# TensorE's order fixed to the program's in the two differential-attention layers of a five-stage fp32 block

## The chip, the cores and the metric

One core of a Trainium2 chip runs the whole program. The metric is the device time of one execution in microseconds (us); lower is better. Batch is 1, the sequence 512 tokens, the model width 1024, all fp32.

## What is computed

Six stages in a row, each adding to the stream `x` (512 x 1024): differential attention, a Conformer convolution, latent attention, differential attention again (with its own weights), a mix of three branches, and a gated feed-forward. The change touches the first and the fourth, which run the same code:

```python
def _diff_attention(h, w_in, q_g, k_g, lq1, lk1, lq2, lk2, sub_g, w_out, lambda_init):
    q, k, v, gate = split(h @ w_in)              # h = rms_norm(x, g)
    q = _apply_rope(_rms_norm(q, q_g), cos, sin) # 8 heads, 2 maps of 64 each
    k = _apply_rope(_rms_norm(k, k_g), cos, sin)
    for s0 in range(0, seq, QBLOCK):             # 4 query blocks of 128
        s = einsum('bhmqd,bhmkd->bhmqk', q[s0:e], k[:e]) * scale
        p = _chunk_causal_softmax(s, s0)
        wts = p[:, :, 0] - lam * p[:, :, 1]
        outs.append(einsum('bhqk,bhkd->bhqd', wts, v[:e]))
    o = _rms_norm(concat(outs), sub_g) * (1.0 - lambda_init)
    return (o * silu(gate)) @ w_out
```

## The kernel before

**Products.** Every large product is made of three fp32r matmuls (`mm3`, L356: high by high, high by low, low by high), each with a moving side of 512 columns. Text below calls one `mm3` a product. A weight unit (512 KB) comes by DMA from the queue of SP (L52), ScalarE rounds it to its high part (L53), and VectorE or GpSimd subtracts to get the low part (L60). Three raw buffers and six pairs of high and low are in turn.

**An attention layer** (`layer_a`, L509) goes through four pairs of heads. For a pair, `project` (L567) first runs the q and k product for four token blocks t = 0 to 3, eight `mm3` each, with the four weight units outside and the token outermost (`tok_outer`), so a token needs all four units. Its result goes through `qk` (L571): a copy and a square on ScalarE (L573, L574), a sum on VectorE (L576), rotary embedding on GpSimd (`rope`, L458 to L461, four instructions), the reciprocal root on GpSimd (L223, L217), and a scaling on VectorE (L580). Only then can `turn` (L582) transpose it on TensorE (four transposes into a PSUM bank `lin`), and ScalarE and VectorE split the result into q and k (L353, L354). A second product gives v and the gate (`vg`, L596). Before its last token, `begin` (L606) asks for all four turns and starts the attention of the pair: for each query block and head the scores (`sc`), the softmax (L637, L638), the transposes of the weights (`weights`, L649), their copy (L652), the values (`values`, L655) and, when both heads are there, `finish` (L668) with two GpSimd instructions (L673, L217) and an output turn (L677). These steps run between the products of the next pair. `out_proj` (L700) multiplies by `w_out`; its last part goes token by token and begins the next layer's norm (`norm`, L325, then `turn`, L341).

**What sets the order.** The program is emitted with the help of `Flow` (L99): a clock that counts matmul columns and a heap of steps with due times. After each `mm3`, `pump` (L115) emits the steps that are due; `need` (L119) emits steps early when something cannot go on without them. Due times are constants: a turn of q and k comes 14 after its token's products in the first pair and 10 + 2t in the others (`A_FIRST`, `A_TURN`), an output turn `A_OUT` = 8.5 after the values, a norm's turn `NORM` = 5 after the norm. A planner that simulates the engines then orders each engine's instructions anew: it takes what it holds to be ready, in order of priority, so that the order emitted is a wish and not a rule. In layer B alone one stretch is kept in the emitted order on TensorE.

PSUM has eight banks: four `lin`, two `tp`, two `sc`. At the start of the kernel seven groups of transposes keep TensorE busy until the first token of `x` has come (`WARM`), and the norms of all four tokens are emitted at once.

Of the kernel before, what the change touches and what calls it, by code (L numbers as in the profile page):

```python
# [13 lines left out]
ALU = mybir.AluOpType  # L14
# [12 lines left out]
NORM = 5.0  # L27
# [3 lines left out]
class WeightStream:  # L31
# [3 lines left out]
    def __init__(self, k, depth, bufs_raw, bufs_hl):  # L35
        self.k, self.depth = k, depth
        self.units, self.made, self.at, self.begun = [], {}, 0, 0
        self.raw = k.ctx.enter_context(k.tc.tile_pool(name="wraw", bufs=bufs_raw))
        self.hl = k.ctx.enter_context(k.tc.tile_pool(name="whl", bufs=bufs_hl))
        self.turn = 0  # L40
# [58 lines left out]
class Flow:  # L99
# [2 lines left out]

    def __init__(self):
        self.clock, self.heap, self.n = 0.0, [], 0

    def later(self, us, fn):
        self.n += 1
        heapq.heappush(self.heap, (self.clock + us, self.n, fn))
# [4 lines left out]
        fn()  # L113

    def pump(self):  # L115
        while self.heap and self.heap[0][0] <= self.clock:
            self._pop()

# [28 lines left out]
class K:  # L147
# [174 lines left out]
            accum_out=self.sums[t][:, b : b + 1],  # L322
        )

    def norm(self, t):  # L325

        nc = self.nc
        x = self.x[:, t]
        s2, ms = self.sums[t], self.stat(1)
        nc.gpsimd.tensor_scalar(out=ms, in0=s2[:, 0:1], scalar1=s2[:, 1:2], scalar2=EPS, op0=ALU.add, op1=ALU.add)  # L330
        r = self.power(ms)
        for b in range(2):
            f = slice(512 * b, 512 * b + 512)
            if b == 1 and t in self.on_pool:
                nc.scalar.activation(out=x[:, f], in_=x[:, f], func=AF.Copy, scale=r)
                nc.gpsimd.tensor_tensor(out=x[:, f], in0=x[:, f], in1=self.gain[:, f], op=ALU.mult)
            else:
                nc.vector.scalar_tensor_tensor(out=x[:, f], in0=x[:, f], scalar=r, in1=self.gain[:, f], op0=ALU.mult, op1=ALU.mult)
        self.flow.later(NORM, lambda: self.turn(t))

    def turn(self, t):  # L341
        if self.newh is None:
# [106 lines left out]
                nc.gpsimd.tensor_tensor(out=cs[:, :, i, a], in0=cos, in1=over(g[:, i, a]), op=ALU.mult)  # L449
                nc.gpsimd.tensor_tensor(out=sn[:, :, i, a], in0=(neg, sin)[half], in1=over(g[:, i, b]), op=ALU.mult)  # L450

    def rope(self, m, raw, tmp, cs, sn, n, groups):

        nc = self.nc
        v = lambda a: a.rearrange("p (i g d) -> p i g d", i=n, g=groups)
        bc = lambda a: a.unsqueeze(2).to_broadcast([P, n, groups, a.shape[-1]])
        rv, mv, tv = v(raw), v(m), v(tmp)
        nc.gpsimd.tensor_tensor(out=tv[..., 0:32], in0=rv[..., 32:64], in1=bc(sn[..., 0:32]), op=ALU.mult)  # L458
        nc.gpsimd.tensor_tensor(out=tv[..., 32:64], in0=rv[..., 0:32], in1=bc(sn[..., 32:64]), op=ALU.mult)
        nc.gpsimd.tensor_tensor(out=mv, in0=rv, in1=bc(cs), op=ALU.mult)  # L460
        nc.gpsimd.tensor_tensor(out=m, in0=m, in1=tmp, op=ALU.add)  # L461

    def add_x(self, n, last=True, scale=1.0, norm=True):
        def consume(t, ps):
# [20 lines left out]
A_SPACE = (1.6, 0.004)  # L485
A_WEIGHTS = (3.5, 0.0065)
A_READY = 1.6
A_OUT = 8.5
A_POOL = 0.3
START_NORM = ()  # L490
WARM = 7
START_LOAD = (2, 5)
A_NORM = (1, 2, 3)


def units_a(ins, j):
    w, wo = ins["a_w_in"][j], ins["a_w_out"][j]
    out = []
    for p in range(4):
        c = 256 * p  # L500
        out += units_tm(w, [(c, 256), (1024 + c, 256)])
        out += units_tm(w, [(2048 + c, 256), (3072 + c, 256)])
    for half in range(2):
        for n in range(2):
            out += units_tm(wo, [(512 * n, 512)], 4 * half, 4)
    return out


def layer_a(k, j, li, gnext, out=None, start=False):  # L509
    nc, tc, ins, flow = k.nc, k.tc, k.ins, k.flow  # L510
    k.share(A_POOL)
    with ExitStack() as ctx:
# [4 lines left out]
        def wt(n, bufs, nmn):  # L517
            return work.tile([P, n], F32, tag=nmn, name=k.nm(nmn), bufs=bufs)

        if start:  # L520

            def between(t):
                if t == 0:
                    k.begin_norm(ins["a_norm_g"][j : j + 1, :], START_NORM)
                    k.share(0.0)
                    k.ws.ahead(START_LOAD[0])
                elif t == 1:
                    k.ws.ahead(START_LOAD[1])
                    k.share(A_POOL)

            k.load_x(between)

            for _ in range(WARM):
                k.transposes([k.ident] * 4)
            for t in range(NT):
                for b in range(2):
                    k.squares(t, b)
                k.norm(t)


        cs = one.tile([P, NT, 2, 64], F32, tag="cs", name=k.nm("cs"))
        sn = one.tile([P, NT, 2, 64], F32, tag="sn", name=k.nm("sn"))
# [24 lines left out]
        def project(p):  # L567

            ks[p] = one.tile([P, 2, 2, S], F32R, tag="ks", name=k.nm("ks"), bufs=2)

            def qk(t, ps):  # L571
                m = wt(512, 4, "m2")
                nc.scalar.activation(out=m, in_=ps, func=AF.Copy)  # L573
                nc.scalar.activation(out=ps, in_=ps, func=AF.Square)  # L574
                ss = k.stat(8)
                nc.vector.tensor_reduce(out=ss, in_=ps.rearrange("p (g d) -> p g d", d=64), axis=AX.X, op=ALU.add)  # L576
                k.rope(m, m, wt(512, 2, "t2"), cs[:, t], sn[:, t], 2, 4)
                r = k.rstd(ss, 64)
                mv = m.rearrange("p (g d) -> p g d", d=64)
                nc.vector.tensor_tensor(out=mv, in0=mv, in1=r.unsqueeze(2).to_broadcast([P, 8, 64]), op=ALU.mult)  # L580

                def turn():  # L582
                    tp = k.transposes([m[:, c * P : (c + 1) * P] for c in range(4)], "lin")
                    s = slice(t * P, (t + 1) * P)
                    q = one.tile([P, 2, 2, 2, P], F32R, tag="qs", name=k.nm("qs"), bufs=4)
                    a, b = slice(0, 64), slice(64, 128)
                    for m_, u, v in ((0, a, b), (1, b, a)):
                        k.split(tp[u, 2:4], ks[p][u, m_, :, s], ks[p][v, m_, :, s])
                        k.split(tp[u, 0:2], q[u, 0, m_], q[u, 1, m_])
                        nc.gpsimd.tensor_copy(out=q[v, :, m_], in_=q[u, :, m_])  # L590
                    qs[p, t] = q
                    turned.add((p, t))

                flow.later(A_FIRST if p == 0 else A_TURN[0] + A_TURN[1] * t, turn)

            def vg(t, ps):  # L596
                vt[p, t] = wt(256, 4, "vt")
                sg[p, t] = wt(256, 4, "sg")
                nc.scalar.activation(out=vt[p, t], in_=ps[:, :256], func=AF.Copy)
                th = wt(256, 2, "th")  # L600
                nc.scalar.activation(out=th, in_=ps[:, 256:], func=AF.Tanh, scale=0.5)
                nc.vector.scalar_tensor_tensor(out=sg[p, t], in0=th, scalar=1.0, in1=ps[:, 256:], op0=ALU.add, op1=ALU.mult)  # L602

            k.lin_tm(k.h_opnd, 8, qk, tok_outer=True, first=p == 0)

            def begin():  # L606
                flow.need(lambda: all((p, t) in turned for t in range(NT)))
                if p % 2 == 0:
                    pair = k.big(F32R, "ot") if p == 0 else one.tile([P, 4096], F32R, tag="ot", name=k.nm("ot"))
                    pair = pair.rearrange("p (i r h t) -> p i r h t", i=2, r=2, h=2)  # L610
                    pairs[p], pairs[p + 1] = [(pair[:, i, 0], pair[:, i, 1]) for i in range(2)]
                    ot[p], ot[p + 1] = [[[pair[:, i, r, h] for h in range(2)] for r in range(2)] for i in range(2)]
                for qt in range(NT):
                    chain.add(attend(p, qt))

            k.lin_tm(k.h_opnd, 8, vg, before_last=begin, tok_outer=True)
            projected.add(p)

        def attend(p, qt):
# [48 lines left out]
            def finish():  # L668
# [16 lines left out]

                flow.later(A_OUT, turn)

# [935 lines left out]
                k.lin_tm(lambda kk: (ah[:, kk], al[:, kk]), 2 * (b - a), k.add_x(n, half == 1, norm=False), tok_outer=half == 1 and n == 1)  # L1623


def build(tc, ctx, ins, out):
    k = K(tc, ctx, ins)
    for u in (
        units_a(ins, 0), units_b(ins, 0), units_c(ins, 0), units_a(ins, 1), units_mix(ins), units_ffn(ins),
    ):  # L1630
        k.ws.add(u)
    layer_a(k, 0, 0.8 - 0.6 * math.exp(-0.3 * 0), ins["b_norm_g"][0:1, :], start=True)
    k.flow.drain()
    layer_b(k, 0, ins["c_norm_g"][0:1, :])
    k.flow.drain()
    layer_c(k, 0, ins["a_norm_g"][1:2, :])
    k.flow.drain()
    layer_a(k, 1, 0.8 - 0.6 * math.exp(-0.3 * 3), ins["norm_mix_2"][0:1, :])
    k.flow.drain()
    layer_mix(k, ins["norm_ffn_2"][0:1, :])  # L1640
    k.flow.drain()
    layer_ffn(k, out)
    k.flow.drain()
# [41 lines left out]
```

## Time and profile before

| | us |
|---|---|
| median of three runs | 2034.39 (2030.29 to 2035.47) |
| the profiled execution | 2031.8 |
| its span, first to last instruction | 2030.0 |
| TensorE busy | 1981.4 (98%) |
| VectorE, ScalarE, GpSimd busy | 1167.4, 997.4, 918.4 |
| granted TensorE clock, mean | 0.995 |

The first attention layer takes the span's first 311 us or so, the second about 751 to 1051. In the rows below PE is TensorE's matmuls, DVE VectorE, ACT ScalarE, POOL GpSimd. A row of the timeline has start, duration, engine, line, operation, output and inputs, and in brackets the idle time of the engine before it with what ended it. Matmuls are pipelined: the pace is the distance between starts, not the duration.

### The profile page before, as it was taken

The page shows a single profiled execution, that of the slowest core. Times are in us where ns is not written, and L with a number is a line of the kernel's source. Part 1 is how long each engine was busy: PE and PEld are TensorE (multiplying, and loading weights), DVE is VectorE, ACT ScalarE, POOL GpSimd, SP SyncE. Part 2 cuts the span into 40 slices and gives each one's busy share as a digit, 9 for nine tenths or more (in the row PEclk, how much of TensorE's full clock was granted, in tenths as well). Part 3 has the DMA queues.
Part 4 walks back from the last instruction along what each step waited for, and adds up shares of the span by engine and source line. Part 5 has one row for each costly group of instructions (what it writes and reads, how often), then busy time and mean ns, then how long its engine had stood idle before and what let it go on. Part 6 is the DMA issues. An engine that isn't in the chain of part 4 may idle for free.

```text
span 2030.0 us, 27252 instructions
## 1 busy us (share of the span) xinstructions
PE 1981.4 (98%) x9875; PEld 1660.1 (82%) x9875; DVE 1167.4 (58%) x2185; ACT 997.4 (49%) x2107; POOL 918.4 (45%) x812
## 2 busy tenths in 40 slices
PE   8899999999999999999999999999999999999999
PEld 7788888877888887878878888888888888888887
DVE  6678766995466656777755678647534333221321
ACT  5556646574466545556544776546423333222220
POOL 6676724993554417775445434102511223333331
PEclk9999999999999999999999999999999999999999
DMA  6122133313331323121432212322334344333321
GB/s 198 51 80 84 55 135 105 114 52 119 116 92 43 104 86 100 61 83 47 141 108 91 65 62 83 94 75 77 119 94 140 94 130 135 98 99 94 104 94 52
DMA packets 161095, 191.54 MB, mean 94 GB/s; under 512 B 15917, under 2 KB 131997, under 8 KB 160960
## 3 DMA queue, kind: packets, MB, share of 16 engines
q1 hardware_dynamic: 160960, 189.80, 29.7%
q8 instruction: 78, 1.28, 0.3%
q14 instruction: 57, 0.47, 0.1%
HBM read 177.18 MB, written 12.58 MB: 93 GB/s over the span
## 4 chain that ended last, share of the span: by engine, by line
PE 83%; DVE 5%; POOL 5%; ACT 3%; issue 2%; DMA 2%; SPq 0%; ACTq 0%; DVEq 0%; POOLq 0%
PE lin L195 73%; PE sc L195 4%; PE tp L195 3%; PE tp L303 2%; PE lin L303 1%; DVE wl L60 1%; POOL st L217 1%; POOL wl L60 1%; DMA wr<-in_a_w_in_dram 1%; ACT wh L53 1%; POOL m L461 1%; POOL m L460 1%; DVE m L580 0%; DMA x<-in_x_dram 0%; DVE st L637 0%
## 5 line engine op out<-in xcount | busy, mean ns | idle before, releaser
L60 POOL TENSOR_TENSOR wl<-wr,wh 128x1024 fp32r<-128x1024 f32 (+2 forms) x151 | 365.1, 2421 | 494.4 <-ACT wh L53 475.5
L53 ACT ACTIVATE wh<-wr 128x1024 fp32r<-128x1024 f32 (+2 forms) x306 | 318.4, 1044 | 372.1 <-PE lin L195 234.1
L195 PE MATMUL lin<-hh,wh 128*128 128x512 f32 (+1 forms) x928 | 349.3, 378 | 1.8 <-ACT hh L353 1.8
L195 PE MATMUL lin<-hl,wh 128*128 128x512 f32 (+1 forms) x928 | 349.9, 377 | 0.0
L195 PE MATMUL lin<-hh,wl 128*128 128x512 f32 (+1 forms) x928 | 349.2, 377 | 0.0
L195 PE MATMUL lin<-wh,hh 128*128 128x512 f32 (+2 forms) x864 | 332.6, 386 | 11.2 <-DVE sg L602 4.5
L195 PE MATMUL lin<-wh,hl 128*128 128x512 f32 (+2 forms) x864 | 330.2, 383 | 0.1
L195 PE MATMUL lin<-wl,hh 128*128 128x512 f32 (+2 forms) x864 | 328.0, 381 | 1.2 <-DVE wl L60 1.0
L60 DVE TENSOR_TENSOR wl<-wr,wh 128x1024 fp32r<-128x1024 f32 (+3 forms) x155 | 213.9, 1383 | 181.1 <-ACT wh L53 180.5
L195 PEld LDWEIGHTS lin<-hh,wh 128*128 128x128 f32 x928 | 175.3, 189 | 33.9 <-ACT hh L353 2.1
L195 PEld LDWEIGHTS lin<-hl,wh 128*128 128x128 f32 x928 | 175.7, 189 | 31.6 <-issue 0.5
L195 PEld LDWEIGHTS lin<-hh,wl 128*128 128x128 f32 x928 | 175.9, 190 | 31.2
L195 PEld LDWEIGHTS lin<-wh,hh 128*128 128x128 f32 x864 | 164.7, 191 | 38.4 <-DVE sg L602 5.6
L195 PEld LDWEIGHTS lin<-wl,hh 128*128 128x128 f32 x864 | 164.4, 190 | 27.9 <-DVE wl L60 2.4
L195 PEld LDWEIGHTS lin<-wh,hl 128*128 128x128 f32 x864 | 164.4, 190 | 26.7 <-DVE hl L354 0.4
L195 PE MATMUL lin<-wh,ot 128*128 128x512 f32 x384 | 129.0, 402 | 2.5 <-ACT ot L680 2.5
L468 DVE TENSOR_TENSOR x<-lin,x 128x512 f32<-128x512 f32 x80 | 54.4, 688 | 114.3 <-PE lin L195 114.2
L217 POOL TENSOR_TENSOR st<-st,minus_half 128x8 f32<-128x8 f32 (+4 forms) x109 | 116.7, 1072 | 6.8 <-DVE st L1159 2.3
L1036 DVE SCALAR_TENSOR_TENSOR tp<-u,taps,tp 128x512 f32<-128x512 f32 x151 | 104.0, 756 | 1.1
L195 PEld LDWEIGHTS lin<-wh,ot 128*128 128x128 f32 x384 | 71.6, 188 | 17.1 <-ACT ot L680 2.9
L1042 POOL TENSOR_TENSOR acc<-acc,tmp 128x512 f32<-128x512 f32 x52 | 66.7, 1300 | 21.9 <-ACT tmp L1040 20.8
L1276 POOL TENSOR_TENSOR merged<-merged,sig 128x512 f32<-128x512 f32 x16 | 22.8, 1430 | 118.0 <-DVE sig L1275 118.0
(327 smaller groups left out, 3851.6 us busy)
## 6 DMA issues: line engine op xcount, KB each, us to landing
wr<-in_a_w_in_dram SPq DMA_DIRECT2D x128, 256.0 KB, 3.1
wr<-in_w_in_dram SPq DMA_DIRECT2D x48, 512.0 KB, 3.7
wr<-in_b_w_in_dram SPq DMA_DIRECT2D x24, 512.0 KB, 4.7
wr<-in_w_branch_dram SPq DMA_DIRECT2D x24, 512.0 KB
wr<-in_w_ffn_gate_dram SPq DMA_DIRECT2D x22, 512.0 KB, 3.8
wr<-in_w_ffn_up_dram SPq DMA_DIRECT2D x22, 512.0 KB, 4.2
wr<-in_w_ffn_down_dram SPq DMA_DIRECT2D x22, 512.0 KB, 3.8
xs<-x SPq DMA_DIRECT2D x40, 256.0 KB, 2.3
```

Source lines behind the costliest of these rows:

```text
L53: nc.scalar.activation(out=hi, in_=raw, func=AF.Copy)
L60: eng.tensor_tensor(out=lo, in0=raw, in1=hi.bitcast(F32), op=ALU.subtract)
L195: self.nc.tensor.matmul(out=out, lhsT=lhsT, rhs=rhs, start=start, stop=stop)
L217: self.nc.gpsimd.tensor_tensor(out=y, in0=ms, in1=self.minus_half.to_broadcast(list(ms.shape)), op=ALU.pow)
L303: self.nc.tensor.transpose(tp[:, c], a, self.ident)
L460: nc.gpsimd.tensor_tensor(out=mv, in0=rv, in1=bc(cs), op=ALU.mult)
L461: nc.gpsimd.tensor_tensor(out=m, in0=m, in1=tmp, op=ALU.add)
L468: self.nc.vector.tensor_tensor(out=xs, in0=ps, in1=xs, op=ALU.add)
L1036: nc.vector.scalar_tensor_tensor(out=ps, in0=tap(u[:, c], i), scalar=wc(i), in1=ps, op0=ALU.mult, op1=ALU.add)
L1042: nc.gpsimd.tensor_tensor(out=acc, in0=acc, in1=tmp, op=ALU.add)
L1276: nc.gpsimd.tensor_tensor(out=merged(i), in0=merged(i), in1=sig[c], op=ALU.add)
```

## The change

- Both attention layers are emitted inside a region in which TensorE's instructions keep the order in which the program emits them. Where they fall among instructions from outside the region, and the order on all other engines, stay the planner's.
- Inside the region `pump` emits due steps only at every second call, so between every six fp32r matmuls and not every three.
- `A_OUT` goes from 8.5 to 11.5.
- At the start of the kernel the norms' turns of tokens 1, 2 and 3 are due 8.5, 13.0 and 17.5 later.
- In the first pair of heads of each attention layer, the last addition of `rope` (L461) goes from GpSimd to VectorE.

```diff
@@ class Flow
         self.clock, self.heap, self.n = 0.0, [], 0
+        self.every, self.asked = 1, 0
...
     def pump(self):
+        self.asked += 1
+        if self.asked % self.every:
+            return
         while self.heap and self.heap[0][0] <= self.clock:
             self._pop()
@@ class K
-    def norm(self, t):
+    def norm(self, t, late=0.0):
...
-        self.flow.later(NORM, lambda: self.turn(t))
+        self.flow.later(NORM + late, lambda: self.turn(t))
...
-    def rope(self, m, raw, tmp, cs, sn, n, groups):
+    def rope(self, m, raw, tmp, cs, sn, n, groups, last=None):
...
-        nc.gpsimd.tensor_tensor(out=m, in0=m, in1=tmp, op=ALU.add)
+        (last or nc.gpsimd).tensor_tensor(out=m, in0=m, in1=tmp, op=ALU.add)
...
-A_OUT = 8.5
+A_OUT = 11.5
...
+START_LATE = (0.0, 8.5, 13.0, 17.5)
@@ layer_a
-                k.norm(t)
+                k.norm(t, START_LATE[t])
...
-                k.rope(m, m, wt(512, 2, "t2"), cs[:, t], sn[:, t], 2, 4)
+                k.rope(m, m, wt(512, 2, "t2"), cs[:, t], sn[:, t], 2, 4, nc.vector if p == 0 else None)
...
+@contextmanager
+def own_order(k):
+
+    k.flow.every = 2
+    with k.tc.manual_schedule(engines={mybir.EngineType.PE}):
+        yield
+    k.flow.every = 1
@@ build
-    layer_a(k, 0, 0.8 - 0.6 * math.exp(-0.3 * 0), ins["b_norm_g"][0:1, :], start=True)
+    with own_order(k):
+        layer_a(k, 0, 0.8 - 0.6 * math.exp(-0.3 * 0), ins["b_norm_g"][0:1, :], start=True)
...
-    layer_a(k, 1, 0.8 - 0.6 * math.exp(-0.3 * 3), ins["norm_mix_2"][0:1, :])
+    with own_order(k):
+        layer_a(k, 1, 0.8 - 0.6 * math.exp(-0.3 * 3), ins["norm_mix_2"][0:1, :])
```

## Rows read from the trace of the kernel before

**Rows 1.** The page: busy time of the engines over the span.
```profile
PE 1981.4 (98%) x9875; PEld 1660.1 (82%) x9875; DVE 1167.4 (58%) x2185; ACT 997.4 (49%) x2107; POOL 918.4 (45%) x812
```

**Rows 2.** Windows of both layers: stretch, length, PE busy (count), granted clock, DMA.
```profile
50.00:68.00 18.00, 12.11 (x52) 0.91 0.08 28
68.00:255.00 187.00, 183.53 (x955) 1.00 0.24 74
300.00:318.00 18.00, 12.93 (x67) 0.96 0.49 161
775.00:803.00 28.00, 23.19 (x102) 0.94 0.24 75
803.00:876.00 73.00, 71.99 (x371) 1.00 0.26 82
876.00:930.00 54.00, 49.05 (x248) 0.97 0.15 46
930.00:1000.00 70.00, 69.29 (x363) 1.00 0.28 92
1040.00:1060.00 20.00, 15.85 (x83) 1.00 0.48 162
```

**Rows 3.** Timeline of PE: the waits that carry most of that idle time.
```profile
54.04 1.08 PE L303 MATMUL lin<-ident,m 128*128 128x128 f32 x4 [3.86 <-DVE m L580]
...
303.52 0.50 PE L195 MATMUL lin<-wh,ot 128*128 128x512 f32 x1 [1.23 <-ACT ot L680]
...
790.61 0.66 PE L303 MATMUL lin<-ident,m 128*128 128x128 f32 x4 [3.59 <-DVE qs L354]
...
892.43 0.50 PE L195 MATMUL lin<-wh,hh 128*128 128x512 f32 x1 [1.63 <-ACT w L638]
...
911.70 0.44 PE L303 MATMUL tp<-ident,og 128*128 128x128 f32 x2 [1.87 <-ACT tp L662]
...
926.11 1.16 PE L195 MATMUL tp<-vt,wT 128*128 128x128 f32 x8 [0.47 <-ACT wT L652]
```

**Rows 4.** Pace at full clock (chain of waits: start, length, count) and behind a wait.
```profile
228.50 4.55 PE lin L195 x20
...
792.35 0.63 PE L195 MATMUL lin<-wl,hh 128*128 128x512 f32 x1
792.77 0.63 PE L195 MATMUL lin<-wh,hl 128*128 128x512 f32 x1
```

**Rows 5.** Timeline of the first 39 us: PE, VectorE, ScalarE.
```profile
7.76 1.33 PE L303 MATMUL tp<-ident,x 128*128 128x128 f32 x8 [0.89 <-PE tp L303]
9.76 0.50 PE L195 MATMUL lin<-wh,hh 128*128 128x512 f32 x1 [0.66 <-ACT hh L353]
...
22.20 1.22 DVE L60 TENSOR_TENSOR wl<-wr,wh 128x1024 fp32r<-128x1024 f32 x1
...
25.65 0.60 ACT L573 ACTIVATE m<-lin 128x512 f32<-128x512 f32 x1
...
26.64 0.61 ACT L573 ACTIVATE m<-lin 128x512 f32<-128x512 f32 x1
```

**Rows 6.** GpSimd and VectorE in `rope` and behind it; the longest third token.
```profile
33.05 1.28 POOL L461 TENSOR_TENSOR m<-m,t 128x512 f32<-128x512 f32 x1
...
L580 DVE TENSOR_TENSOR m<-m,st x32: 666/693/2889, 36.0 to 979.1; 128x512 f32<-128x512 f32 x32
...
890.20 0.59 ACT L573 ACTIVATE m<-lin 128x512 f32<-128x512 f32 x1
...
907.52 2.89 DVE L580 TENSOR_TENSOR m<-m,st 128x512 f32<-128x512 f32 x1
```

**Rows 7.** The last values of the first layer, and their scaled output on VectorE.
```profile
297.11 1.95 PE L195 MATMUL tp<-vt,wT 128*128 128x128 f32 x16
...
300.94 0.43 DVE L675 TENSOR_TENSOR og<-og,st 128x256 f32<-128x256 f32 x1 [1.49 <-POOL st L217]
```

## The prediction

> **What bounds the kernel now.** I read the page first: TensorE is busy for 98% of the span and no other engine comes near that [rows 1]. So nothing that is saved on another engine counts by itself. The change adds no matmul and takes none away; it can only move the time in which TensorE waits, and the time for which it then runs at the lower clock. The next view is the windows of the two layers. Length less busy time gives the idle time of each stretch: 5.9 us at 50 to 68, 3.5 at 68 to 255, 5.1 at 300 to 318, and in the second layer 4.8 at 775 to 803, 1.0 at 803 to 876, 4.9 (4.95) at 876 to 930, 0.7 at 930 to 1000 and 4.1 (4.15) at 1040 to 1060, together 30.0 us [rows 2]. Four of these stretches have a granted clock under 1: 0.91 of 18 us, 0.96 of 18, 0.94 of 28 and 0.97 of 54, which is 1.6 + 0.7 + 1.7 + 1.6 = 5.6 us of clock. Then the timeline shows how the two go together: after a wait of 3.59 us the matmuls start 0.42 us apart where the full pace is 4.55 / 20 = 0.2275 us, so they run at 1.2 GHz in place of 2.4 [rows 3, 4]. 35.6 us, or 1.8%, is all that a better order can win in these layers.
>
> The waits have one look: TensorE stands before a transpose or a product whose operand is still in a queue of VectorE, ScalarE or GpSimd, while products that could run stand behind it [rows 3]. The planner put that instruction there because in its own simulation the operand was ready. The program's order places the same steps by fixed due times. The question is whether those due times are longer than the latencies of the chip.
>
> **The change part by part.**
>
> *How long the due times are.* `Flow` counts 512 / 2400 = 0.213 us for a matmul that takes 0.2275, so its time runs 1.07 times as long on the chip. A q and k turn of the first pair then comes 14 x 1.07 = 15 us after its product, a third turn of a later pair (10 + 2 x 2 = 14) also 15, a fourth 17; emission at every sixth matmul only adds up to 6 x 0.2275 = 1.4. An output turn moves from 8.5 x 1.07 = 9.1 to 12.3 us. The longest third turn of the six later pairs needed 907.52 + 2.89 - 890.20 = 20.2 us [rows 6], though in a stretch where TensorE's own order had bunched the work. I take 15.5 us as the lead that the fixed order gives.
>
> *The start of the first layer, first pair: 0 us (from -3 to +6.7).* The fixed order must finish token 0 before token 1. Token 0 needs the fourth weight unit, whose low part ends at 22.20 + 1.22 = 23.4; six matmuls later it is 24.8. Now the late turn of token 1 comes; from the start of such a turn to the first product were 9.76 - 7.76 = 2.0 us, then 24 matmuls take 5.5 and the turn of token 2 in between about 0.9 (at most 1.3, the row's length): 33.2. Before, the planner let both tokens go forward on the units that were there, and both were copied out by 26.64 [rows 5], the product itself being done at about 26.5. So the fixed order is 6.7 us behind. What it gets back is the stretch 50 to 68: 5.9 us idle and about 1 us of clock. There TensorE waited for token 2's scaled q and k [rows 3], because two tokens had arrived on GpSimd at once; in the new order they arrive about 5.5 + 0.9 = 6.4 us apart, and GpSimd loses one instruction of 1.28 us per token [rows 6]. 6.7 - 6.9 is nothing.
>
> *The added work on VectorE.* Four additions in each of two layers go from GpSimd, at 1.28 us, to VectorE. The nearest row there is the scaling of L580, the same shape with two inputs in SBUF: 0.69 us at the median, 2.89 at most [rows 6]. 8 x 0.69 = 5.5 us on an engine that is busy 58% of the time; I put it at nothing, covered by the 15 us of lead. Behind the waiting addition stand the splits of earlier turns, so if that cover is gone the price is a wait like the one at 790.61 [rows 3].
>
> The row's largest value is over four times its median. The Trainium skill ("SBUF — State Buffer", section "SBUF: two separate sides") says that VectorE with two SBUF inputs and GpSimd share a port pair that one holds for a whole instruction while the other is blocked. By that rule the move frees GpSimd of 1.28 - 0.69 = 0.6 us for each token and not of 1.28; the spread of the row speaks for it, and the third rival below is what it would do here.
>
> *The second layer, first pair: -5 us (0 to -6.4).* Idle 4.8 us and 8 matmuls at 0.43 in place of 0.23, 1.6 us, are behind the wait of 3.59 us [rows 2 to 4]. The turn that stood there will come 15 us after its product. I leave 1.4 us for shorter waits.
>
> *The second layer, third pair: -5 us (0 to -6.5).* Here the waits of 1.63 and 1.87 us [rows 3] and the low clock between them. The second of them is an output turn, for which the lead grows by 3.2 us, more than the 1.87 that it missed.
>
> *The other pairs: 0 us (-5.2 to the first rival's price).* 3.5 + 1.0 + 0.7 us are idle there today. The fixed order will have short waits of its own; I let them cancel.
>
> *The ends of the layers: -5.1 us (-10 to 0).* 5.1 idle and 0.7 clock, and 4.1. The fixed order has the attention done earlier and the last product token by token, 24 matmuls or 5.5 us apart, so the next norms hide behind products and the following layer starts without waiting. What stays: the last output turn, whose operand is ready 300.94 + 0.43 - (297.11 + 1.95) = 2.3 us after the values [rows 7] and before which only six matmuls and another output turn, 1.6 us, are emitted, so 0.7; the copy behind it, 1.23 [rows 3]; and half a us for a norm, an estimate. 5.8 - 2.4 = 3.4 and 4.1 - 2.4 = 1.7 make 5.1.
>
> *New waits: +3.8 us (0 to +8).* Several steps now come one behind the other without products between them, above all the copy of the weights that the values need; one such wait was 0.47 us [rows 3]. One in each of eight pairs.
>
> Sum: 0 + 0 - 5 - 5 + 0 - 5.1 + 3.8 = -11.3 us. Of the profiled execution's 2031.8 us that leaves 2020.5; the median of the runs is 2.6 above that execution, so 2023.1, rounded to 2023.
>
> **The rivals.**
>
> *Slower: the third turn is late and now holds all.* Today a late turn costs little where the planner has put other products ahead of it; in the fixed order all products wait. At the longest latency the wait is 20.2 - 15.5 = 4.7 us, with 1.6 for the clock 6.3. Two such pairs in six eat the forecast's gain; that is the point, or a mean third latency above 15.5 + 11.3 / 6 = 17.4 us. With three pairs and the short waits of the start at 2 us it is 2023 + 18.9 = 2042. For it: GpSimd carries rotary embedding, roots, copies of q and a third of the low parts in one queue. Against it: tokens will come in more evenly, and each pair holds only one such turn.
>
> *The start is not paid back.* The fourth token's chain still ends late and TensorE waits at the end of the first pair as at 54.04: 2023 + 6.7 = 2029.7.
>
> *The additions on VectorE block it.* If they take 2.9 us rather than 0.69 and hold the splits behind them, the second layer's first pair keeps its wait and the first layer's gets half of one: 2023 + 5 + 3 = 2031.
>
> *It changes little.* The planner's order is the program's in most places, and what differs is not what waits: 2032 to 2034. Against it: two tokens finished within 1 us of each other at the start [rows 5], which the program's order never does.
>
> **How the numbers follow.** The forecast has 0.58, the slower rival 0.14, the start 0.12, the additions 0.10, no effect 0.06. About 0.3% (6 us) is what a measurement of this kernel can tell from no change, so faster means under 2028.3. The forecast nearly always, and a part of the start rival, lie there: 0.62. Between 2028.3 and 2040.5 lie the rest of the start, the additions and no effect, 0.24; above, 0.14. The range goes down to 2008, where the short waits do not come and the pairs and the ends give nearly all that they can, 15 us below the forecast, and up to 2038, which takes in three rivals and the slower one with two pairs and a little.
>
> **What would show it.** Right: in the profile after, the stretches 775 to 803 and 876 to 930 have no wait over 1 us and full clock; the first pair's products end a few us later and 50 to 70 is without idle; the first product of the layer behind each attention layer starts without waiting. Wrong: TensorE waits for `m` (L580) or for a split before a third or fourth turn, in several pairs, or for weights at the start of a token 0 beyond the first one; or the idle time of the two layers is still about 30 us in other places. A change of several us in the layers that were not touched would also make it wrong, for the planner runs over the whole program.

## The result: slower by 1%, where faster by 0.6% was forecast

| | before | after |
|---|---|---|
| median of four runs each, side by side (us) | 2034.93 | 2052.47 (2050.77 to 2055.02) |
| ratio to before, 95% interval | | 1.0096 [1.008, 1.0111] |
| span of the profiled execution | 2030.0 | 2048.9 |
| mean granted clock of TensorE | 0.995 | 0.992 |

The time lies above the forecast's range of 2008 to 2038, and it moved the other way. The page of the kernel after, busy time of the engines (before: [rows 1]):

```profile
PE 1988.7 (97%) x9875; PEld 1661.0 (81%) x9875; DVE 1180.1 (58%) x2193; ACT 1001.7 (49%) x2107; POOL 903.3 (44%) x804
```

The matmuls are the same 9875. The span grew by 18.9 us: TensorE's idle time went from 2030.0 - 1981.4 = 48.6 to 2048.9 - 1988.7 = 60.2, which is 11.6, and its busy time grew by 7.3 for the same work, because more of it ran at the lower clock (by the granted clock 0.8% of 2049 us below full speed, 16 us, against 0.5% of 2030, 10). In the two attention layers alone the idle time went from 29.7 to 42.9 us.

To see where, I took two kinds of marks from the timelines of both kernels: the start of ScalarE's last copy of values in a pair (L604 after, L599 before) and of the last addition to the stream in a layer (L472, L468; in the second attention layer at 1076.0 after, 1052.8 before). All lines of the kernel after lie four or five below those of before. Each mark is read from one profiled execution. What a stretch adds, after less before:

| stretch | forecast | measured |
|---|---|---|
| start and first pair, first layer | 0 | -2.2 |
| its other three pairs | 0 | +2.3, +4.2, +2.4 |
| its end; what layers B and C give back | -3.4 | +8.4; -2.4 |
| first pair, second layer | -5 | -4.5 |
| its second, third and fourth pair | 0, -5, 0 | +4.9, -2.2, +5.2 |
| its end; what the rest gives back | -1.7 | +7.2; -4.3 |
| new waits anywhere | +3.8 | in the rows above |
| sum | -11.3 | +18.9 |

The waits of TensorE in the kernel after, first for 0 to 330 us, then for 760 to 1060 (what waited, for what; us in total, times, longest):

```profile
PE tp L307 <- DVE w L650: 4.9, 3, 2.9
PE lin L199 <- DVE wl L60: 4.7, 3, 2.2
PE tp L307 <- DVE ot L686: 3.2, 3, 1.6
PE sc L199 <- ACT w L643: 2.8, 3, 1.5
...
PE tp L307 <- ACT tp L667: 8.3, 3, 3.1
PE tp L307 <- DVE w L650: 2.9, 3, 1.1
PE tp L307 <- DVE og L680: 2.4, 1, 2.4
```

The waits of before that carried the forecast, for `m` (L580) and for the splits of q and k [rows 3], are gone. In the second layer's first pair one of 1.88 us is left (797.13, for VectorE's sum L581, which stands behind a scaling L585 of 2.88 us). For the rest, in their place stand waits for attention's own steps: the softmax weights (L650, L643), a bank that ScalarE has not emptied (L667), the operands of the output turns (L680, L686), and at the start the weight units (L60, L53). The single waits of some length, from the timeline of TensorE (the bracket has the idle time before and what ended it):

```profile
16.22 0.50 PE L199 MATMUL lin<-wl,hh 128*128 128x512 f32 x1 [2.19 <-DVE wl L60]
20.36 0.79 PE L199 MATMUL lin<-wh,hh 128*128 128x512 f32 x1 [2.50 <-ACT wh L53]
23.40 0.79 PE L199 MATMUL lin<-wl,hh 128*128 128x512 f32 x1 [2.24 <-DVE wl L60]
...
262.97 0.47 PE L307 MATMUL tp<-ident,w 128*128 128x128 f32 x1 [2.88 <-DVE w L650]
...
302.20 0.41 PE L307 MATMUL tp<-ident,og 128*128 128x128 f32 x2 [2.55 <-DVE og L680]
...
338.60 1.11 PE L307 MATMUL tp<-ident,x 128*128 128x128 f32 x4 [3.45 <-POOL x L340]
...
839.37 0.55 PE L307 MATMUL tp<-ident,w 128*128 128x128 f32 x3 [3.12 <-ACT tp L667]
...
904.38 0.62 PE L307 MATMUL tp<-ident,w 128*128 128x128 f32 x3 [2.92 <-ACT tp L667]
...
968.73 0.55 PE L307 MATMUL tp<-ident,w 128*128 128x128 f32 x3 [2.23 <-ACT tp L667]
```

The wait at 839.37 recurs in the next two pairs (904.38, 968.73). Its chain, from the timelines of TensorE, VectorE and ScalarE of the kernel after:

```profile
834.77 0.38 PE L307 MATMUL tp<-ident,og 128*128 128x128 f32 x2
...
835.42 0.83 PE L199 MATMUL tp<-vt,wT 128*128 128x128 f32 x6
...
834.17 1.09 DVE L650 SCALAR_TENSOR_TENSOR w<-w,st 128x384 f32<-128x384 f32 x1
835.18 0.68 DVE L581 TENSOR_REDUCE st<-lin 128x8 f32<-128x512 f32 x1
...
836.01 1.29 DVE L642 TENSOR_REDUCE st<-sc 128x1 f32<-128x512 f32 x2
...
836.74 0.69 ACT L643 ACTIVATE w<-sc,st 128x512 f32<-128x512 f32 x1 [2.83 <-DVE st L642]
...
837.41 0.68 ACT L643 ACTIVATE w<-sc,st 128x512 f32<-128x512 f32 x1
...
838.08 0.47 ACT L685 ACTIVATE ot<-tp,subg 128x256 fp32r<-128x256 f32 x1
...
838.95 0.26 ACT L667 ACTIVATE tp<-tp 128x128 f32<-128x128 f32 x1
```

An output turn (834.77) and the values (835.42) take the two `tp` banks within 0.7 us, and the next transposes, due at once, want one of them. ScalarE, which has to read both before they are free (a scaled copy, L685, and the squares of the values, L667), stands before an exponential whose maximum (L642) is queued on VectorE behind L650 and L581; it sat idle for 2.83 us with these two behind the exponentials in its queue. TensorE is stopped for 3.12 us, and soon after its clock is halved, as after the 3.59 us of before [rows 4]: from 839.4 to 844.0 the granted clock is 0.63 (last section).

### The profile page after: what moved, and what is told of

It reads as the page before. It is cut to its first block, busy times and chain, and to the rows that moved or that the text cites. A ratio compares the mean times of both kernels' runs of the same rounds, so it can differ in the third digit from the quotient of the medians.

```text
span 2048.9 us, 27217 instructions
## 1 busy us (share of the span) xinstructions
PE 1988.7 (97%) x9875; PEld 1661.0 (81%) x9875; DVE 1180.1 (58%) x2193; ACT 1001.7 (49%) x2107; POOL 903.3 (44%) x804
## 3 DMA queue, kind: packets, MB, share of 16 engines
q8 instruction: 78, 1.28, 0.3%
## 4 chain that ended last, share of the span: by engine, by line
PE 83%; DVE 7%; ACT 3%; POOL 3%; DMA 2%; issue 2%; SPq 0%; ACTq 0%; POOLq 0%; DVEq 0%
PE lin L199 73%; PE sc L199 4%; PE tp L199 3%; PE tp L307 2%; DVE wl L60 1%; PE lin L307 1%; DVE st L642 1%; POOL wl L60 1%; ACT w L643 1%; DMA wr<-in_a_w_in_dram 1%; POOL st L221 1%; ACT wh L53 1%; DMA xs<-x 1%; DVE w L650 1%; DVE st L649 0%
## 5 line engine op out<-in xcount | busy, mean ns | idle before, releaser
L60 POOL TENSOR_TENSOR wl<-wr,wh 128x1024 fp32r<-128x1024 f32 (+2 forms) x151 | 364.3, 2417 | 481.3 <-ACT wh L53 475.6
L53 ACT ACTIVATE wh<-wr 128x1024 fp32r<-128x1024 f32 (+2 forms) x306 | 319.3, 1044 | 376.2 <-PE lin L199 230.5
L199 PE MATMUL lin<-wh,hh 128*128 128x512 f32 (+2 forms) x864 | 339.1, 393 | 5.0 <-ACT wh L53 2.5
L60 DVE TENSOR_TENSOR wl<-wr,wh 128x1024 fp32r<-128x1024 f32 (+3 forms) x155 | 213.5, 1379 | 183.9 <-ACT wh L53 183.3
L199 PE MATMUL lin<-wh,ot 128*128 128x512 f32 x384 | 133.7, 410 | 2.5 <-ACT w L643 2.4
L221 POOL TENSOR_TENSOR st<-st,minus_half 128x2 f32<-128x2 f32 (+4 forms) x109 | 116.5, 1071 | 7.3 <-DVE st L1164 2.3
L472 DVE TENSOR_TENSOR x<-lin,x 128x512 f32<-128x512 f32 x80 | 54.4, 688 | 112.0 <-PE lin L199 111.4
L643 ACT ACTIVATE w<-sc,st 128x128 f32<-128x128 f32 (+3 forms) x96 | 50.4, 527 | 62.9 <-DVE st L642 62.5
L595 POOL CAST qs<-qs 64x512 fp32r<-64x512 f32 x64 | 49.2, 769 | 63.4 <-DVE qs L358 59.3
```

Of the source, the lines that this page charges most:

```text
L53: nc.scalar.activation(out=hi, in_=raw, func=AF.Copy)
L60: eng.tensor_tensor(out=lo, in0=raw, in1=hi.bitcast(F32), op=ALU.subtract)
L199: self.nc.tensor.matmul(out=out, lhsT=lhsT, rhs=rhs, start=start, stop=stop)
L221: self.nc.gpsimd.tensor_tensor(out=y, in0=ms, in1=self.minus_half.to_broadcast(list(ms.shape)), op=ALU.pow)
L472: self.nc.vector.tensor_tensor(out=xs, in0=ps, in1=xs, op=ALU.add)
L643: nc.scalar.activation(out=e[:, m, :n], in_=sc[:, :n], func=AF.Exp, bias=mx[:, m : m + 1], accum_out=sums[:, 2 * m + h : 2 * m + h + 1],)
```

## The experiments

Every run stands beside runs of the kernel before; differences in us are the ratio less one, times 2032. `every` counts questions of `pump`, one after each `mm3`; where an expectation speaks of three or six products it means single matmuls, so 2 is "six" and 1 is "three". "By the marks" means the marks of the table above, against the kernel before unless another is named.

**The order alone: the kernel after with the planner ordering TensorE.**

```diff
     k.flow.every = 2
-    with k.tc.manual_schedule(engines={mybir.EngineType.PE}):
-        yield
+    yield
     k.flow.every = 1
```

> The changed kernel without the region: the planner orders TensorE again, and the later output turns, the later first turns, the steps at every second product and the moved addition stay. Theory 1 (two tp banks in a fixed order): nothing waits in place, since the planner puts products ahead of a turn whose bank is held, so 2030 to 2038 us, as the kernel before. Rival (the due times and the moved addition cost by themselves): above 2044.

Measured: 2023.72, ratio 0.9961 [0.9946, 0.9976]. The other edits together win 8 us, which is below theory 1's 2030 to 2038. The fixed order, which the forecast credited with the gain, costs (1.0096 - 0.9961) x 2032 = 27 us (21 to 34 by the ends of the two intervals).

**Smaller bunches: steps between every three matmuls.**

```diff
-    k.flow.every = 2
+    k.flow.every = 1
```

> The changed kernel with steps between every three matmuls again, region kept. Counted along the emitted order, the second head's transpose of the third query block comes 1.1 us behind the values that hold the other tp bank, as with every six. Theory 1 (the output turn at 11.5 brings three users of two tp banks together): the waits stay, 2047 to 2056. Rival (emitting at every second product bunches the steps and makes the waits): half of the loss goes, about 2043.

Measured: 2038.05, 1.0034 [1.0022, 1.0047], 13 us less than the kernel after. Its waits in the second layer, and below them in the first:

```profile
PE tp L307 <- DVE w L650: 4.4, 3, 2.9
PE sc L199 <- ACT w L643: 2.3, 3, 1.1
...
PE tp L307 <- DVE w L650: 6.0, 3, 2.9
PE lin L199 <- DVE wl L60: 5.0, 3, 2.5
PE sc L199 <- ACT w L643: 3.6, 3, 2.3
...
833.65 0.52 PE L307 MATMUL tp<-ident,w 128*128 128x128 f32 x3 [0.51 <-DVE ot L686]
```

The 8.3 us for L667 are gone. The last line, from the timeline of TensorE, is the step that waited 3.12 us at 839.37. TensorE still runs the output turn (831.66), the values, a turn of q and k and these transposes one behind the other; what has moved is that three matmuls now stand between the transposes before them and the scores, where both came together. ScalarE takes up the first exponential as the output turn starts (831.71; in the kernel after 2 us behind it), and the wait is 0.51 us. The waits for the softmax and for weight units stay. By the marks 8.6 of the 12.9 us between the two profiled executions come in the second layer's last three pairs and 6.4 in the layers B and C, whose code is the same; the first layer ends 2.7 us later. Why B and C gain is not shown.

**Is it the bank? Output turns into a `lin` bank in the first three pairs.**

```diff
-                    tp = k.transposes([og[:, h] for h in range(2)])
+                    tp = k.transposes([og[:, h] for h in range(2)], "lin" if p < 3 else "tp")
```

> The changed kernel with the output turns of pairs 1 to 3 in a lin bank in place of a tp bank, so that two tp banks serve only the weights' transposes and values. Theory 1: the waits of a weights' transpose for ACT L667 and DVE L686, 12.1 us in six places and three stretches of low clock of about 1.6 us behind them, go: 2036 to 2041. Rival (in a fixed order the softmax is late and the bank is only the last name on the list): the same waits for DVE L650 take their place, 2048 to 2053.

Measured: 2051.3, 1.0093 [1.0078, 1.0109], no change from the kernel after. Its waits in the second layer:

```profile
PE lin L307 <- ACT w L643: 4.5, 3, 1.6
PE lin L307 <- DVE og L680: 3.3, 3, 1.8
```

The waits for L667 are gone here too, but the same steps now stop at the next thing that is late: the output turn at a `lin` bank that an exponential still reads (three times), or at its own operand (three times). So another bank alone wins nothing: the bank is where the lateness showed, and the fixed order meets the next late thing instead. Spacing the steps did take these waits away.

**Is it the later output turn? The kernel after with output turns due at 8.5.**

```diff
-A_OUT = 11.5
+A_OUT = 8.5
```

Expected were 2046 to 2056 (steps that are emitted together hold the few banks against each other), or as the rival 2035 to 2041 (the output turn at 11.5 makes the waits). There is no time: in this order steps wait for each other in a circle, a deadlock, so the question stays open for the fixed order. Which steps form the circle is not shown.

**The fixed order for the first pair only, output turns as before.**

```diff
-A_OUT = 11.5
+A_OUT = 8.5
...
-            project(p)
+            if p == 0:
+                with own_order(k):
+                    project(p)
+            else:
+                project(p)
```

(The whole-layer regions in `build` are taken out.)

> The region and the step every six matmuls around the first pair of heads of each attention layer alone, the planner for all else, output turns due at 8.5 as before; late first turns and the moved addition stay. Between the kernels the first pair's last gate product came 2.2 us earlier in the first layer and 4.5 us earlier (12.7 late before it, 8.2 behind it) in the second. Theory 1: these 6.7 us stay won, 2026 to 2031. Rival (what a pair wins is given back by the next, whose steps come from a planner with another plan): 2032 to 2037.

Measured: 2025.71, 0.9967 [0.9956, 0.9977], which is the 6.7 us of theory 1. But the later runs give the moved addition by itself 0.9919; with the order fixed in the first pair, its steps at every second question and the late norm turns it is 0.0048 or 10 us worse. So the gain is not the order's.

**The ends: the region closed ahead of `out_proj`.**

```diff
-        for p in range(4):
-            if p >= 2:
-                flow.need(lambda: attended(p - 2))
-            project(p)
+        with own_order(k):
+            for p in range(4):
+                if p >= 2:
+                    flow.need(lambda: attended(p - 2))
+                project(p)
```

(The regions in `build` are taken out.)

> The changed kernel with the region ended ahead of the output product of each attention layer, so that the planner orders the last pair's output turns, the output product and the next norm's turns. From the last gate product to the last addition the changed kernel lost 8.4 us in the first layer and 8.0 in the second, and the layers behind gave back 3.5 and 5.2. Theory: the net 7.7 us come back and some of the wait for the last output turn with it, 2040 to 2046. Rival (the loss sits in the pairs, and a tail that the planner orders starts as late): 2049 to 2053.

Measured: 2042.12, 1.0049 [1.0032, 1.0067], 10 us less. By the marks the ends cost +4.2 and +3.3 in place of +8.4 and +7.2, so in the fixed order the end of each layer loses and does not win. (The 8.0 and 5.2 of the expectation belong to the last addition of the output product's first half, and its 3.5 to layer B alone.) What is left is near what the planner has: with it and all other edits the ends cost +2.7 and +4.0, with the moved addition alone 0.0 and +0.2, and with that and the later output turns (below) +2.6 and +3.7.

**Both of these undone.** (Steps between every three matmuls, region closed ahead of `out_proj`.)

> The kernel after with both undone that paid singly: steps between every three products instead of six (2038), and the region closed ahead of out_proj (2042); the later output turns, the moved addition and the fixed order up to the last gate products stay. If the two losses are separate (bunches of six in the second layer, the hand-over to out_proj at both ends) they add up: 2052 - 14 - 10, so 2025 to 2031, near the 2024 that the same edits take with the planner; then little is left that is the fixed order's own. If both runs won back the same waits: 2035 to 2040. If the fixed order costs in itself, wherever the steps stand: 2036 or more, with the waits for the first scores' softmax still there.

Measured: 2036.82, 1.0022 [1.0012, 1.0033]: 15 us better than the kernel after, where 13 and 10 came singly, so the two won back partly the same time. The time lies in the ranges of the second and of the third theory, and both have a part: (1.0022 - 0.9961) x 2032 = 12 us stay the fixed order's own. (Steps come at every second question in the kernel with 0.9961; the one with every question, the moved addition and the later output turns has 0.9965, below.) By the marks 11 of them are there when the first layer's fourth pair ends. Its waits in the first layer:

```profile
PE lin L199 <- DVE wl L60: 4.9, 3, 2.4
PE tp L307 <- DVE ot L686: 4.6, 4, 3.3
PE sc L199 <- ACT w L643: 3.3, 2, 2.3
PE tp L307 <- DVE w L650: 3.1, 2, 2.3
```

These four are 15.9 us together. The two largest of the kernel with the planner's order, 0 to 330 us:

```profile
PE tp L307 <- DVE ot L686: 3.3, 1, 3.3
PE lin L307 <- DVE m L585: 3.2, 1, 3.2
```

The four largest are 10.9 there, and weight units and the softmax are not among them. Up to the last addition of the first layer TensorE is idle for 24.0 us in the fixed order and for 17.4 with the planner's.

**The late norm turns alone, in the kernel before.**

```diff
-                k.norm(t)
+                k.norm(t, (0.0, 8.5, 13.0, 17.5)[t])
```

> The kernel before with the late first norm's turns alone, no region. The changed kernel without its region came out at 2023.7 against 2031.3, and in it the first pair ended 4.9 us earlier. Theory A (the late turns keep the tokens apart, so that GpSimd's chain is not met by two at once): 2024 to 2028. Theory B (the moved addition does it): 2030 to 2033.

Measured: 2031.51, 0.9998 [0.9988, 1.0008]: no change, theory B. By the marks the first pair does end 4.7 us earlier, but 2.8 of them are lost again by the end of the fourth: what a pair wins did not reach the end of the kernel.

**The moved addition alone, in the kernel before.**

```diff
-        nc.gpsimd.tensor_tensor(out=m, in0=m, in1=tmp, op=ALU.add)
+        (last or nc.gpsimd).tensor_tensor(out=m, in0=m, in1=tmp, op=ALU.add)
...
-                k.rope(m, m, wt(512, 2, "t2"), cs[:, t], sn[:, t], 2, 4)
+                k.rope(m, m, wt(512, 2, "t2"), cs[:, t], sn[:, t], 2, 4, nc.vector if p == 0 else None)
```

> The kernel before with the moved addition alone, in the first pair of both layers, no region. Theory B: GpSimd's queue is 1.28 us shorter for each of four tokens, the wait of 3.9 us at 54 and that of 3.6 us at 791 go, 2021 to 2027. Theory A: VectorE's queue gets what GpSimd's loses, 2029 to 2034.

Measured: 2015.36 (2013.48 to 2019.08), 0.9919 [0.99, 0.9938]: 16 us faster than before (13 to 20 by the interval), and by its median the fastest kernel of this study. Its page, the group of the moved additions and of those left on GpSimd, and the two waits of the first pairs:

```profile
PE 1973.4 (98%) x9875; PEld 1655.5 (82%) x9875; DVE 1176.2 (58%) x2193; ACT 995.2 (49%) x2107; POOL 914.1 (45%) x804
...
L461 DVE TENSOR_TENSOR m<-m,t 128x512 f32<-128x512 f32 x8 | 5.5, 693 | 8.0 <-POOL m L460 7.9
...
L461 POOL TENSOR_TENSOR m<-m,t 128x512 f32<-128x512 f32 x24 | 32.9, 1370 | 0.6
...
51.61 0.63 PE L303 MATMUL lin<-ident,m 128*128 128x128 f32 x4 [2.23 <-DVE qs L354]
...
776.65 0.50 PE L195 MATMUL lin<-wh,hh 128*128 128x512 f32 x1 [2.04 <-DVE st L576]
```

An addition costs 1.37 us on GpSimd and 0.69 on VectorE. The gain is larger than either theory had. In the first pair of the first layer the wait is 2.23 us where it was 3.86, in that of the second 2.04 where it was 3.59 [rows 3]. In the profiled execution the span is 18.3 us shorter: 10.3 of idle time (48.6 to 2011.7 - 1973.4 = 38.3) and 8.0 of busy time that ran at the lower clock before. By the marks 6.6 and 5.4 us of it come in the two first pairs, 2.0 in the layers B and C, and 5.3 in the second layer's third pair, where no addition was moved; there the planner put the steps otherwise, and why is not shown.

**The addition put back in the kernel after.**

```diff
-                k.rope(m, m, wt(512, 2, "t2"), cs[:, t], sn[:, t], 2, 4, nc.vector if p == 0 else None)
+                k.rope(m, m, wt(512, 2, "t2"), cs[:, t], sn[:, t], 2, 4, None)
```

> The kernel after, with rope's last addition of the first pairs back on GpSimd; all else of the change stays. Beside the planner this addition moved to VectorE was worth some 18 us (2015.4 against 2033). If the fixed order has to wait for the same chain of GpSimd at the head of each layer, the two add up: 2052 + 14 to 20, so 2066 to 2072, with the first values' end at +3 to +6 to before instead of -2.2. If the fixed order's other waits (banks, output turns) cover that chain, the addition is worth little here: 2050 to 2058.

Measured: 2058.83, 1.0141 [1.0126, 1.0156]; the addition is worth 9 us in the fixed order, between the two theories. The timeline of TensorE, first pairs of the first and the second layer:

```profile
63.62 0.66 PE L307 MATMUL lin<-ident,m 128*128 128x128 f32 x4 [1.09 <-DVE m L585]
...
806.54 1.08 PE L307 MATMUL lin<-ident,m 128*128 128x128 f32 x4 [4.47 <-DVE qs L358]
```

In the first layer the fixed order does nearly without the wait by itself (1.09 us in place of 3.86), as forecast. In the second it does not: 4.47 us, longer than before. Its chain starts on GpSimd: VectorE stands idle for 2.56 us until GpSimd's addition is done, its scaling (L585, 800.55) then takes 2.85 us beside a low part on GpSimd, and the split that TensorE needs (L358, ending at 806.40) stands behind it.

**What of the planner's 2015 is lost again by the rest: later output turns, and steps at every second question, each with the moved addition in the kernel before.**

```diff
-A_OUT = 8.5
+A_OUT = 11.5
```

> The kernel before with the moved addition and output turns planned 3 us later (A_OUT 11.5), the planner orders TensorE. Moved addition alone was 2015.4, with later output turns and steps at every second product 2023.7: 8 us lie between. If the later output turns cost it (they leave the last output turns and out_proj with less ahead): 2020 to 2025 here. If the steps at every second product cost it: 2013 to 2017 here and the 8 us in the run beside it.

Measured: 2022.91, 0.9965 [0.9953, 0.9977]. The later output turns cost 0.46% or 9 us of the addition's gain. By the marks, against the moved addition alone, they lose 4.4 and 2.3 us in the first layer's third and fourth pair, 2.0 in the second layer's fourth and 2.6 and 3.5 at the two ends, and 5.5 come back behind the second layer.

```diff
+        self.asked += 1
+        if self.asked % self.every:
+            return
```

(With `every` = 2 through both attention layers.)

> The kernel before with the moved addition and the plan's steps let in only at every second question, the planner orders TensorE; output turns as before. If bunching of the steps costs the 8 us between 2015.4 and 2023.7 also without the fixed order: 2020 to 2025 here. If later output turns cost them: 2013 to 2017. If each costs a part, both runs lie between 2017 and 2021.

Measured: 2020.32, 0.9949 [0.9931, 0.9967], which overlaps the interval of the addition alone; 6 us at the middle, not settled. With both and the late norm turns it was 0.9961, so by the middles the losses don't add.

**The addition moved in all pairs.**

```diff
-2, 4, nc.vector if p == 0 else None)
+2, 4, nc.vector)
```

> The kernel before with rope's last addition on VectorE in all pairs, 32 additions in place of 8. If the addition only matters where the first scores of a layer wait for GpSimd's queue, the other 24 change nothing: 2013 to 2018. If GpSimd's chain also stands behind the waits at the third pair and the ends of the layers: 2005 to 2011. If VectorE, the busier engine there, has to pay for them (24 x 0.4 us = 10 us of work): 2018 to 2026.

Measured: 2021.4, 0.995 [0.9936, 0.9965]. The other 24 additions win nothing and by the middle cost 6 us; the intervals just touch. VectorE's busy time grew from 1176.2 to 1189.9, and whether that is the cause is not shown.

## Why the prediction was wrong, step by step

**What bounds the kernel: right.** Waits, with the lower clock behind some of them, were the whole matter: 11.6 and 7.3 us in the kernel after, -10.3 and -8.0 in the one with the moved addition, with the same 9875 matmuls.

**The start of the first layer, 0: right, by its own steps.** The first pair's last q and k was copied 8.6 us later and the second token's 8.0 (34.64 for 26.64; 6.7 had been worked out), and the stretch after it, where a third of 18 us had been idle [rows 2], came out full. From the windows of the kernel after (stretch, length, busy, granted clock, DMA):

```profile
0.00:46.90 46.90, 37.07 (x161) 0.89 0.56 176
46.90:71.60 24.70, 24.70 (x120) 1.00 0.33 103
```

What the step left out is the comparison: the planner with the same moved addition wins 6.6 us in this stretch without paying at the start. With the addition put back the fixed order, with the late norm turns, has -1.1 here, so its own part is near the 0 that was worked out.

**The added work on VectorE, 0: the term that was missed.** Its price was right; the additions took 0.69 us each. Its gain was not asked for. The forecast itself had a GpSimd queue behind the wait at 54.04 and "one instruction of 1.28 us per token" less, and booked the win to the order. The runs give 16 us to the addition beside the planner. The third rival, additions that last 2.9 us, did not occur: the eight have a mean of 0.69 us in that kernel, and of 6.4 / 8 = 0.80 in the kernel after. The Trainium skill's rule that was weighed there ("SBUF — State Buffer", section "SBUF: two separate sides"), one holder of the shared ports at a time, would not forbid this gain, only shrink what GpSimd saves. The trace of the moved addition alone agrees: beside two of the eight additions an instruction of GpSimd that takes 0.20 us (the median of L223) took 0.69.

```profile
31.42 0.69 DVE L461 TENSOR_TENSOR m<-m,t 128x512 f32<-128x512 f32 x1 [1.38 <-POOL m L460]
...
31.48 0.69 POOL L223 TENSOR_SCALAR st<-st 128x8 f32<-128x8 f32 x1
```

The other such pair stands at 758.75 and 758.80, and beside a third addition (53.77) a copy of 0.61 us (L590) took 1.04. The five others ran beside the root (L217), which took 1.63 to 1.65 us as it does without them (1.65 at 768.43 in the kernel before). So GpSimd lost about 0.5 us three times in eight, not 0.7 each time.

**The second layer, first pair, -5: right number, wrong reason.** It measured -4.5, but with the addition put back the fixed order has its wait of 4.47 us there, and the stretch is 1.0 us longer than before. The order gave nothing: the third token's turn came 20.1 us after its copy (786.47 to 806.54), so the lead of 15.5 us did not cover GpSimd's chain, and the first rival's wait of 4.7 us is what stood there.

**The third pair, -5, and the other pairs, 0: wrong.** -2.2 for the third, and +2.3 to +5.2 for each of the five others. The failing step is "The fixed order will have short waits of its own; I let them cancel." They do not cancel: by the windows of these stretches TensorE is idle for 7.9 us in the first layer's last three pairs (3.5 before) and for 10.5 in the second's (6.7 before). And they are not short: the largest are 1.0 to 1.6 us in the first layer and 2.2 to 3.1 in the second, there with the clock behind them.

**The ends, -5.1: wrong in sign.** +8.4 and +7.2, of which the following layers gave back 2.4 and 4.3. With the planner the later output turns alone cost some 3 us at each end; in the forecast they only gain. The 2.88 us at 262.97 lie in this stretch too. The step took over 0.7 us before the last output turn; in the kernel after it was 2.55 (302.20) and, in the second layer, 2.44. In the first layer its operand was ready 4.0 us after the values, not 2.3, because the low part of a weight unit stands ahead of it on GpSimd:

```profile
298.30 2.37 POOL L60 TENSOR_TENSOR wl<-wr,wh 128x1024 fp32r<-128x1024 f32 x1 [10.26 <-ACT wh L53]
300.63 0.19 POOL L678 TENSOR_TENSOR st<-st,st 128x2 f32<-128x2 f32 x1
```

The next layers' first products did start without a wait, as forecast (in the kernel before 1.82 us at 314.49 and 2.92 at 1055.24). But in layer B the last token's transposes waited 3.45 us (338.60): ScalarE's scaling ahead of them (L339) had stood 6.36 us until a DMA that reads `x` had ended, a term that the forecast lacks.

**New waits, +3.8 at one of 0.47 us in each pair: the size that failed.** The steps were priced as if only their own latency counted. What the trace shows is queues: a square of 0.26 us (L667) started 2.7 us after the values that it reads (838.95 for 836.25), behind two exponentials that waited for VectorE. Ahead of the last pair's weights in the first layer the low parts of the weight units do the same. VectorE's timeline of the kernel after:

```profile
257.10 2.09 DVE L60 TENSOR_TENSOR wl<-wr,wh 128x1024 fp32r<-128x1024 f32 x1 [0.50 <-ACT wh L53]
...
261.44 1.21 DVE L60 TENSOR_TENSOR wl<-wr,wh 128x1024 fp32r<-128x1024 f32 x1
262.57 0.34 DVE L650 SCALAR_TENSOR_TENSOR w<-w,st 128x128 f32<-128x128 f32 x1
```

Two low parts, 2.09 and 1.21 us, stand with some short instructions ahead of L650, and TensorE waits 2.88 us for it (262.97). No due time in `Flow` sees these queues. With the planner's order the same edits have no wait of 0.25 us or more for L667, and for L650 one of 1.4 us in both layers together; that its simulation of the queues is the reason was not tried by itself.

**The slower rival, 2042: nearest in time, wrong in place.** Its mechanism, that what is late now holds everything, is what happened. Its operand, the third turn of q and k, held TensorE only with the addition put back (4.47 us). In the kernel after it is not what waits: no wait for L585 or for a split is among the leading ones of the kernel after, and the late ones are the softmax, the banks and the output turns. Its chance of 0.14 was too low for the same reason as the term above: one late step in a pair was counted, where every step of the attention between two products can be the late one. (Two of the forecast's sums are off and change nothing: its idle times add up to 30.1, not 30.0, and the rival's 18.9 is three pairs at 6.3 without the 2 us of short waits that it names.)

What stays open: by which waits the planner loses 9 us with later output turns, why the addition wins in the third pair of the second layer, why the layers that were not touched give time back, and what a fixed order over whole layers costs with earlier output turns, for with 8.5 it deadlocks.

## What to carry to other kernels

Here an order fixed by hand on the engine that bounds the kernel turned late operands on other queues into stops of everything, and with one other due time it could not run at all. Before fixing such an order, look in the trace for all steps between two products, with the queue that each result stands in, and not only for the step that waits today. Where a wait names a chain on another engine, shorten that chain first: one instruction per token in the first pairs, moved to the engine that does it in half the time, won 16 us where the fixed order lost 27. In a bundle of edits, price the small ones for what they gain as well as for what they cost, and time them singly.

## What the runs showed of the hardware

Whether the half clock follows a wait is not told by the wait's length alone. Windows of the kernel after (stretch, length, busy, granted clock, DMA), behind the wait of 2.55 us that ended at 302.20 and behind the one of 3.12 that ended at 839.37:

```profile
302.30:306.00 3.70, 3.70 (x18) 1.00 0.46 162
...
839.40:844.00 4.60, 4.60 (x17) 0.63 0.00 0
```

After the first the clock stayed full; in the kernel with the moved addition a wait of 2.23 us (51.61) was followed by matmuls 0.43 us apart from 53.09 on. And it can last: at the start of the kernel after, with waits of 2.19, 2.50 and 2.24 us between 14.0 and 23.4, the matmuls are 0.42 to 0.43 us apart (1.2 GHz in place of 2.4) still after the third wait, and the granted clock of the first 46.9 us is 0.89.

```profile
24.00:25.70 1.70, 1.70 (x6) 0.50 0.66 208
```

So a wait can cost its length alone or its length and some us of clock (behind 839.37, 4.6 us at 0.63 are 1.7 us), and the forecast's price of its new waits, by the length, was too low for those of the second layer.
